# Delta rule: dealing the rows of a block's inverse out in turn over the partition groups

## The chip, the cores and the metric

The kernel runs on one core of one Trainium2 chip. The metric is the device time of one launch in microseconds (us); the runs shown agree within about 0.3%. Engines are called by the profile's names: PE (matrix products), DVE (vector), ACT (scalar), POOL (GpSimd) and SP, which here issues nearly all DMAs. PEld is PE's loading of weights.

## The reference

One layer of a hybrid encoder is applied to 512 prompt tokens and to eight requests of 16 tokens, 640 rows in all, in fp32. Each row goes through one wide input projection, then through two branches: forgetting attention with 8 heads, and a gated delta rule with 8 heads of 128 x 128 state. Both branches are projected, gated, merged, normalised and gated once more. The part that the change touches is the solve in the delta rule, per head and block of tokens:

```python
lmat = jnp.where(strict, jnp.einsum('nbhid,nbhjd->nbhij', kb, kc) * decay, 0.0)
amat = lmat + jnp.eye(c, dtype=lmat.dtype)
solve = functools.partial(lax.linalg.triangular_solve, left_side=True, lower=True)
u = solve(amat, vc * bc[..., None])
w = solve(amat, kb * jnp.exp(gc)[..., None])
```

`amat` is unit lower triangular. The kernel forms its inverse explicitly and multiplies by it.

## The kernel before, in words

**Stages.** The program has four stages: a front (input projection of the attention part and of gates), the attention stage, the delta-rule stage, and a tail (output projections, norm, last gate). In the profile the delta-rule stage runs from about 990 to 1600 us. PE is fed all the time by wide products: 128 x 128 weights against 320 columns, three products for one fp32 product (a high and a low part of each operand), recorded by `column` (L396, L397) and `pair` (L474). Between these, the heads' small products are slipped in, with PSUM tiles called `s`; the wide ones write tiles called `g`.

**One head of the delta rule** is a chain of Python generators. `gdn` (L901) transposes, normalises and forms `lt`, the scaled and masked key products (L974 on PE, L979 on DVE). `gdn_blocks` (L988) inverts the 32 x 32 blocks on the diagonal, 20 blocks a head (5 tiles of 128 tokens by 4). `gdn_feed` (L1015) reads the inverses back. `gdn_merge` (L1028) builds the 128 x 128 inverse `uu` from four blocks with small products (L1043, L1051, L1057, L1066, L1072; the DVE copies L1052, L1060 and L1074 lie between them). `gdn_chunks` (L1079) then runs the recurrence over the prompt's four tiles (`gdn_pro`, L1178: L1196 uses `uu`; L1188 and L1210 use the state `S`, which DVE writes in L1206; L1192 forms the right side `rp`) and the update of the eight requests (`gdn_dec`, L1132). `gdn_out` normalises and stores.

**The substitution (L1002 to L1008).** `lt`'s diagonal blocks are written to a DRAM tile `ld` (L993, four DMAs of 32 x 5 x 32), then read back as `lanes` (L998): a block's whole matrix, 1024 numbers, on each of four partitions, so 20 blocks fill 80 partitions. `x` (tile `sx`, 8 rows of 32 per partition) starts as the identity from an input `eye` (L996). A block has 32 rows of inverse; the four partitions of a block hold eight rows each: rows 0 to 7, 8 to 15, 16 to 23 and 24 to 31. Step j takes column j out of all eight slots with a multiply and a subtract (L1004, L1006): 31 steps, 62 DVE instructions a head. Row r of the inverse has nothing in column j before j reaches r, so many of these products are zeros. One DMA writes `x` to `xd` (L1012); `gdn_feed` reads it back as `u0`, 32 partitions per block (L1023, tile `u`). POOL copies it into `uu` (L1033), DVE transposes it into `m0` (L1035, tile `m`), and the merge begins with L1043 on PE.

**What sets the order.** Every engine runs its instructions in the order in which the kernel records them; the scheduler does not move them. The order is set while the kernel is written out, by a planner with a cost model. `saw` (L81) watches each recorded instruction and keeps a modelled clock for PE and a modelled time at which DVE, ACT and POOL are done: for DVE 0.17 us and 1.1 ns an element. After every few wide products `tick` (L125) lets each lane's generator go on, if its `yield` count of ticks has passed and the modelled time of what it recorded last lies behind the modelled clock of PE. So the number of elements in a DVE instruction decides how many wide products are recorded before the next piece of a head's chain. `yield -1` (L1008), after every second step of the substitution, lets the lane go on a little before DVE is done.

**Who else stands in these queues.** SP issues the weight loads (`wr`, L269), the sums of weights (`ws`, L291 and L301) and every head's loads. In this stage POOL issues the DMAs that complete the low part of the weights (`wl`, L342), between its copies. ACT makes `wh` and the negated high part.

Of the kernel before, what the change touches and what calls it, by code (L numbers as in the profile page):

```python
# [14 lines left out]
ALU = mybir.AluOpType  # L15
# [37 lines left out]
class Kernel:  # L53
# [934 lines left out]
    def gdn_blocks(self, h, kq, lt, qk, qg, kt, vr, cs):  # L988

        nc = self.nc  # L990
        for a in range(4):
            sl = slice(32 * a, 32 * a + 32)
            nc.sync.dma_start(out=self.ld[:, a].rearrange("t j i -> j t i"), in_=lt[sl, :, sl])  # L993
        yield 5
        x = self.zt([80, 8, 32], "sx")
        nc.sync.dma_start(out=x.rearrange("p c i -> p (c i)"), in_=self.i["eye"])  # L996
        lanes = self.zt([80, 32, 32], "lanes")
        nc.sync.dma_start(out=lanes.rearrange("p j i -> p (j i)"),  # L998
                          in_=bass.AP(self.ld.tensor, self.ld.offset, [[1024, 20], [0, 4], [1, 1024]]))
        yield 5  # L1000
        tmp = self.zt([80, 8, 32], "sx2")
        for j in range(31):  # L1002
            n = 31 - j
            nc.vector.tensor_tensor(out=tmp[:, :, 0:n], in0=x[:, :, j:j + 1].to_broadcast([80, 8, n]),  # L1004
                                    in1=lanes[:, j:j + 1, j + 1:32].to_broadcast([80, 8, n]), op=ALU.mult)
            nc.vector.tensor_tensor(out=x[:, :, j + 1:32], in0=x[:, :, j + 1:32], in1=tmp[:, :, 0:n], op=ALU.subtract)  # L1006
            if j % 2 == 1:
                yield -1  # L1008
        self.inv = h
        while self.fed < h - 2:  # L1010
            yield
        nc.sync.dma_start(out=self.xd[h % 2], in_=x.rearrange("p c i -> p (c i)"))  # L1012
        self.feeds["gens"].append(self.gdn_feed(h, kq, lt, qk, qg, kt, vr, cs))

    def gdn_feed(self, h, kq, lt, qk, qg, kt, vr, cs):  # L1015
# [1317 lines left out]
def _consts():  # L2333
    cb = np.zeros((P, C_N), np.float32)
    i = np.arange(P)
    blk = i // 16
    same = blk[:, None] == blk[None, :]
    le = i[None, :] <= i[:, None]
    cb[:, C_ID:C_ID + P] = np.eye(P)
    cb[:, C_MP:C_MP + P] = np.where(le, 0.0, NEG)  # L2340
    cb[:, C_MD:C_MD + P] = np.where(le & same, 0.0, NEG)
    cb[:, C_DP:C_DP + P] = np.where(le.T, 0.0, NEG)
    cb[:, C_DD:C_DD + P] = np.where(le.T & same, 0.0, NEG)
    cb[P - 1, C_SP:C_SP + P] = 1.0
    cb[:, C_SD:C_SD + P] = (i[:, None] % 16 == 15) & same
    cb[:, C_ONE:C_ONE + P] = 1.0
    cb[:, C_EO:C_EO + 2] = blk[:, None] % 2 == np.arange(2)[None, :]
    cb[:, C_S4:C_S4 + 32] = (i[:, None] % 32) == np.arange(32)[None, :]
    cb[:, C_G4:C_G4 + 4] = i[:, None] == 32 * np.arange(4)[None, :]
    smask = np.ones((32, T), np.float32)  # L2350
    t = np.arange(T)
    smask[0:8, (t >= NPT) & (t % 16 == 0)] = 0.0
    smask[8:16, ((t < NPT) & (t % P == 0)) | ((t >= NPT) & (t % 16 == 0))] = 0.0
    smask[16:32] = 0.0
    eye = np.zeros((20, 4, 8, 32), np.float32)
    for c in range(4):
        for j in range(8):
            eye[:, c, j, 8 * c + j] = 1.0
    return cb, smask, eye.reshape(80, 256)


def _layout(a):
# [43 lines left out]
    for b in gate[Kernel.GATES:]:  # L2406
# [24 lines left out]
    rowb[0:8, 3], rowb[8:32, 3] = 1.0, -1.0  # L2431
    rowb = np.tile(rowb, (4, 1))
    cb, smask, eye = _consts()
    arr = {"w": w, "xT": x.T.reshape(KT, P, T), "pT": pp.T.reshape(2, P, T),
           "wsm": wsm.reshape(KT, P, 32).transpose(1, 0, 2), "kc": kc, "vc": vc, "lfr": lfr, "conv": conv,
# [38 lines left out]
```

## Time and profile before

| what | value |
|---|---|
| time, median of 3 runs | 2175.85 us (2170.36 to 2176.83) |
| the profiled execution's own time | 2173.18 us |
| its span, first to last instruction | 2171.3 us |
| granted TensorE clock, mean | 0.999 |
| PE busy | 2149.0 us, 99% of the span |
| DVE busy | 1566.0 us, 72% |
| ACT busy | 1007.3 us, 46% |
| POOL busy | 401.9 us, 19% |
| DMA | 452.65 MB, 208 GB/s in the mean |

The table's first rows are times of whole launches; the rows under them come from one profiled execution. "Busy" is the share of the span in which an engine ran an instruction. Idle time counts only on the engine that bounds the kernel.

### The profile page before, as it was taken

How to read it: one execution, taken by the hardware profiler on the slowest of the kernel's cores; microseconds unless marked ns; L12 is line 12 of the kernel's file. 1: busy time of each engine (PE TensorE's matmuls, PEld its weight loads, DVE VectorE, ACT ScalarE, POOL GpSimd, SP SyncE). 2: the span in 40 equal slices, each digit the busy share in tenths (PEclk: the TensorE clock that was granted, in tenths of full speed). 3: DMA queues.
4: the chain of work that ended last, by engine and by line, in shares of the span. 5: the costliest groups of instructions: out<-in, count | busy, mean ns of one | idle time of the engine just before them, and what ended most of it. 6: DMA issues, size and time to landing. Idle time of an engine off the chain costs nothing.

```text
span 2171.3 us, 41951 instructions
## 1 busy us (share of the span) xinstructions
PE 2149.0 (99%) x15438; PEld 2082.3 (96%) x15438; DVE 1566.0 (72%) x3207; ACT 1007.3 (46%) x2213; POOL 401.9 (19%) x596
## 2 busy tenths in 40 slices
PE   9999999999999999999999999999999999999998
PEld 7799999999999998899999999999999999999998
DVE  5877776767776565566478677766757787789987
ACT  4344443443444343353655566655443343354544
POOL 0022233323330101002334333332000000021100
PEclk9999999999999999999999999999999999999999
DMA  6356656666554899869978778878567656673465
GB/s 235 101 184 202 189 182 199 198 199 194 184 180 158 276 325 344 314 199 291 241 179 199 180 188 194 189 182 248 161 229 260 209 171 202 201 276 122 153 227 173
DMA packets 240670, 452.65 MB, mean 208 GB/s; under 512 B 38920, under 2 KB 122504, under 8 KB 240464
## 3 DMA queue, kind: packets, MB, share of 16 engines
q1 hardware_dynamic: 224912, 421.64, 59.5%
q0 software_dynamic: 15552, 28.32, 8.0%
q8 instruction: 122, 2.00, 0.4%
q14 instruction: 84, 0.69, 0.1%
HBM read 353.48 MB, written 96.38 MB: 207 GB/s over the span
## 4 chain that ended last, share of the span: by engine, by line
PE 91%; DVE 3%; DMA 3%; ACT 1%; SPq 0%; issue 0%; POOL 0%; ACTq 0%; DVEq 0%; POOLq 0%
PE g L474 44%; PE g L396 18%; PE g L397 18%; PE g L440 2%; PE s L974 1%; PE s L742 1%; PE s L813 1%; PE s L773 1%; DMA ws138b<-ws 0%; PE s L440 0%; PE s L1168 0%; DMA nb<-rd 0%; DVE sx L1006 0%; DVE sx L1004 0%; PE s L726 0%
## 5 line engine op out<-in xcount | busy, mean ns | idle before, releaser
L329 ACT CAST wh<-wr 128x512 fp32r<-128x512 f32 x624 | 381.2, 619 | 288.7 <-PE g L474 109.5
L335 DVE TENSOR_TENSOR wl<-wr,wh 128x512 fp32r<-128x512 f32 x516 | 358.3, 708 | 183.5 <-ACT wh L329 173.7
L474 PE MATMUL g<-xh,wh 128*128 128x320 f32 (+1 forms) x1296 | 402.9, 311 | 2.7 <-ACT m L1278 1.6
L474 PE MATMUL g<-xl,wh 128*128 128x320 f32 (+1 forms) x1296 | 401.2, 310 | 0.6 <-DVE xl L371 0.6
L474 PE MATMUL g<-xh,wl 128*128 128x320 f32 (+1 forms) x1296 | 401.4, 310 | 0.0
L396 PE MATMUL g<-xh,wh 128*128 128x320 f32 (+1 forms) x960 | 313.0, 326 | 0.7 <-ACT wh L329 0.7
L396 PE MATMUL g<-xh,wl 128*128 128x320 f32 (+1 forms) x960 | 297.1, 309 | 0.8 <-DMA wl<-in_w 0.7
L396 PE MATMUL g<-xl,wh 128*128 128x320 f32 (+1 forms) x960 | 297.2, 310 | 0.4 <-DVE xl L371 0.4
L397 PE MATMUL g<-xh,wh 128*128 128x320 f32 x960 | 297.3, 310 | 0.0
L397 PE MATMUL g<-xl,wh 128*128 128x320 f32 x960 | 297.0, 309 | 0.0
L397 PE MATMUL g<-xh,wl 128*128 128x320 f32 x960 | 296.7, 309 | 0.0
L474 PEld LDWEIGHTS g<-xh,wh 128*128 128x128 f32 x1296 | 243.9, 188 | 4.3 <-ACT m L1278 2.1
L474 PEld LDWEIGHTS g<-xl,wh 128*128 128x128 f32 x1296 | 243.7, 188 | 1.1 <-DVE xl L371 1.1
L474 PEld LDWEIGHTS g<-xh,wl 128*128 128x128 f32 x1296 | 244.1, 188 | 0.0
L474 PE MATMUL g<-t,wh 128*128 128x320 f32 (+1 forms) x1088 | 241.4, 310 | 0.0
L335 DVE TENSOR_TENSOR wl<-sr,wh 128x512 fp32r<-128x512 f32 x200 | 147.9, 759 | 98.6 <-ACT wh L329 97.6
L295 POOL TENSOR_TENSOR ws<-ws 128x171 f32<-128x171 f32 (+2 forms) x152 | 116.7, 768 | 541.5 <-DMA ws<-in_w 535.7
L396 PEld LDWEIGHTS g<-xh,wh 128*128 128x128 f32 x960 | 180.9, 188 | 11.9 <-issue 7.1
L474 PEld LDWEIGHTS g<-t,wh 128*128 128x128 f32 x1088 | 181.9, 188 | 0.6 <-issue 0.3
L396 PEld LDWEIGHTS g<-xh,wl 128*128 128x128 f32 x960 | 180.6, 188 | 1.4 <-DMA wl<-in_w 1.0
L397 PEld LDWEIGHTS g<-xh,wh 128*128 128x128 f32 x960 | 181.0, 189 | 0.9
L396 PEld LDWEIGHTS g<-xl,wh 128*128 128x128 f32 x960 | 180.9, 188 | 1.0 <-DVE xl L371 1.0
(440 smaller groups left out, 4148.8 us busy)
## 6 DMA issues: line engine op xcount, KB each, us to landing
wr<-in_w SPq DMA_DIRECT2D x252, 512.0 KB
wl<-in_w POOLq DMA_DIRECT2D x108, 256.0 KB, 5.8
kc<-in_kc SPq DMA_DIRECT2D x32, 512.0 KB
vc<-in_vc SPq DMA_DIRECT2D x32, 512.0 KB
sr<-in_w SPq DMA_DIRECT2D x25, 512.0 KB
ws<-in_w SPq DMA_DIRECT2D x96, 128.0 KB
sb<-in_w SPq DMA_DIRECT2D x80, 128.0 KB
md<-m SPq DMA_DIRECT2D x32, 320.0 KB
```

The lines of the kernel that those rows point to most:

```text
L295: nc.gpsimd.tensor_tensor(out=o, in0=x, in1=y, op=op)
L329: nc.scalar.copy(out=hi, in_=src)
L335: nc.vector.tensor_tensor(out=lo, in0=src, in1=hi.bitcast(F32), op=ALU.subtract)
L396: nc.tensor.matmul(ps[0], whl[w], xhl[o][:, a], start=(first and x == 0), stop=(last and x == 2))
L397: nc.tensor.matmul(ps[1], whl[w], xhl[o][:, b], start=(first and x == 0), stop=(last and x == 2))
L440: nc.tensor.matmul(ps, x[:, sl], w, start=(s == 0 and n == 0), stop=(s == 15 and n == 2))
L474: nc.tensor.matmul(ps, a[:, w], b, start=(k == 0 and n == 0 and not more), stop=(k == last and n == 2), skip_group_check=True)
L742: nc.tensor.matmul(ops[:, 0:P], vn[:, kb, :], pT[:, kb * P:(kb + 1) * P], start=(kb == 0), stop=(kb == i))
L773: nc.tensor.matmul(s1[32 * j:32 * j + 32, :], self.qpad[:, 2 * j + par, :], kc[:, (j % 2) * NPT:(j % 2 + 1) * NPT], start=(par == 0), stop ...
L813: nc.tensor.matmul(od[32 * j:32 * j + 32, 0:P], self.ppad[:, c, 2 * j + par, :], vc[:, o:o + P], start=False, stop=(par == 1 and c == 3), ...
L974: nc.tensor.matmul(pp[:, o:o + 256].rearrange("p (a b) -> p a b", a=2), kq[:, 0, x], kq[:, :, x], start=True, stop=True)
```

## The change

Row r of a block's inverse moves from partition group r // 8, slot r % 8, to group r % 4, slot r // 4. The rows are dealt out in turn. Then, in step j, the rows that have begun (r <= j) fill the first j // 4 + 1 slots in every group, and the two DVE instructions treat only these slots. The count of instructions stays at 62 a head. The elements per partition of one pass over the 31 steps go from 8 x 496 = 3968 to 1560 (a sum of (j // 4 + 1) x (31 - j)).

The partitions are ordered group first, then block, so that each group's 20 partitions lie together. The identity in `eye` and the pattern with which `lanes` is read follow that. `xd` keeps its layout in DRAM (a block's 32 rows in order), so what reads it is unchanged; but since a partition's slots are now every fourth row, the write takes four DMAs, one a group, each with 160 pieces of 32 numbers (128 B), instead of one with 80 rows of 1 KB.

```diff
-                          in_=bass.AP(self.ld.tensor, self.ld.offset, [[1024, 20], [0, 4], [1, 1024]]))
+                          in_=bass.AP(self.ld.tensor, self.ld.offset, [[0, 4], [1024, 20], [1, 1024]]))
         yield 5
         tmp = self.zt([80, 8, 32], "sx2")
         for j in range(31):
             n = 31 - j
-            nc.vector.tensor_tensor(out=tmp[:, :, 0:n], in0=x[:, :, j:j + 1].to_broadcast([80, 8, n]),
-                                    in1=lanes[:, j:j + 1, j + 1:32].to_broadcast([80, 8, n]), op=ALU.mult)
-            nc.vector.tensor_tensor(out=x[:, :, j + 1:32], in0=x[:, :, j + 1:32], in1=tmp[:, :, 0:n], op=ALU.subtract)
+            m = j // 4 + 1
+            nc.vector.tensor_tensor(out=tmp[:, 0:m, 0:n], in0=x[:, 0:m, j:j + 1].to_broadcast([80, m, n]),
+                                    in1=lanes[:, j:j + 1, j + 1:32].to_broadcast([80, m, n]), op=ALU.mult)
+            nc.vector.tensor_tensor(out=x[:, 0:m, j + 1:32], in0=x[:, 0:m, j + 1:32], in1=tmp[:, 0:m, 0:n],
+                                    op=ALU.subtract)
             if j % 2 == 1:
                 yield -1
         self.inv = h
         while self.fed < h - 2:
             yield
-        nc.sync.dma_start(out=self.xd[h % 2], in_=x.rearrange("p c i -> p (c i)"))
+        xd = self.xd[h % 2]
+        for a in range(4):
+            nc.sync.dma_start(out=bass.AP(xd.tensor, xd.offset + 32 * a, [[1024, 20], [128, 8], [1, 32]]),
+                              in_=x[20 * a:20 * a + 20])
...
-    eye = np.zeros((20, 4, 8, 32), np.float32)
+    eye = np.zeros((4, 20, 8, 32), np.float32)
     for c in range(4):
         for j in range(8):
-            eye[:, c, j, 8 * c + j] = 1.0
+            eye[c, :, j, 4 * j + c] = 1.0
```

The planner's model counts fewer elements, so from the first head's substitution on it records the instructions of the delta-rule stage in another order; before that and after that stage the order is the same on every engine, and each PE instruction is there as often as before. Three places are shown. Rows give the source line, the operation, the tiles (out<-in) and the shape. In the changed kernel's rows the lines of the substitution are one higher than before (L1005 and L1007 for L1004 and L1006), and the lines behind it five higher (L1079 for L1074).

**DVE, head 5's merge.** The row for L1074 is the copy that completes `uu` of head 5; above it stand steps of head 6's substitution, whose first waits for `lanes`. Before:

```order
L1004 TENSOR_TENSOR sx_17586<-sx,lanes 80x8x25
L1006 TENSOR_TENSOR sx<-sx,sx_17586 80x8x25
L1004 TENSOR_TENSOR sx_17586<-sx,lanes 80x8x24
L1006 TENSOR_TENSOR sx<-sx,sx_17586 80x8x24
L880 SCALAR_TENSOR_TENSOR cy<-strip,taps,cy 128x664
L1004 TENSOR_TENSOR sx_17586<-sx,lanes 80x8x23
L1006 TENSOR_TENSOR sx<-sx,sx_17586 80x8x23
L1004 TENSOR_TENSOR sx_17586<-sx,lanes 80x8x22
L1006 TENSOR_TENSOR sx<-sx,sx_17586 80x8x22
L1074 TENSOR_SCALAR uu_11303<-s 64x4x64
```

The same place in the changed kernel:

```order
L1005 TENSOR_TENSOR sx_17546<-sx,lanes 80x2x25
L1007 TENSOR_TENSOR sx<-sx,sx_17546 80x2x25
L1005 TENSOR_TENSOR sx_17546<-sx,lanes 80x2x24
L1007 TENSOR_TENSOR sx<-sx,sx_17546 80x2x24
L1005 TENSOR_TENSOR sx_17546<-sx,lanes 80x3x23
L1007 TENSOR_TENSOR sx<-sx,sx_17546 80x3x23
L1005 TENSOR_TENSOR sx_17546<-sx,lanes 80x3x22
L1007 TENSOR_TENSOR sx<-sx,sx_17546 80x3x22
L1079 TENSOR_SCALAR uu_11303<-s 64x4x64
```

In both kernels ten steps of head 6, 20 instructions, stand between head 5's L1060 and L1074. They are narrower now, and two convolution steps (L880) that stood among them before have moved ahead of the merge.

**DVE, head 7's substitution begins.** Its first step waits for `lanes`; splits of weights and operands (L335, L371) and the recurrence of head 6 (L1192, L1206) stand between its steps. Before:

```order
L1004 TENSOR_TENSOR sx_18608<-sx,lanes 80x8x31
L1006 TENSOR_TENSOR sx<-sx,sx_18608 80x8x31
L1004 TENSOR_TENSOR sx_18608<-sx,lanes 80x8x30
L1006 TENSOR_TENSOR sx<-sx,sx_18608 80x8x30
L1192 SCALAR_TENSOR_TENSOR rp<-s,negc,vr 128x128
L335 TENSOR_TENSOR wl<-wr,wh 128x512
L371 TENSOR_TENSOR xl<-ogr,xh 128x640
L1004 TENSOR_TENSOR sx_18486<-sx,lanes 80x8x29
L1006 TENSOR_TENSOR sx<-sx,sx_18486 80x8x29
```

In the changed kernel:

```order
L1197 SCALAR_TENSOR_TENSOR rp<-s,negc,vr 128x128
L1005 TENSOR_TENSOR sx_18568<-sx,lanes 80x31
L1007 TENSOR_TENSOR sx<-sx,sx_18568 80x31
L1005 TENSOR_TENSOR sx_18568<-sx,lanes 80x30
L1007 TENSOR_TENSOR sx<-sx,sx_18568 80x30
L335 TENSOR_TENSOR wl<-wr,wh 128x512
L371 TENSOR_TENSOR xl<-ogr,xh 128x640
L1005 TENSOR_TENSOR sx_18568<-sx,lanes 80x29
L1007 TENSOR_TENSOR sx<-sx,sx_18568 80x29
L1005 TENSOR_TENSOR sx_18568<-sx,lanes 80x28
L1007 TENSOR_TENSOR sx<-sx,sx_18568 80x28
L1211 SCALAR_TENSOR_TENSOR S<-S,gl,s 128x128
```

The first step now stands behind L1192 (L1197), and the state update L1206 (L1211) stands behind the first four steps. How far a load stands ahead of its first use has changed too. In the order in which the kernel records its instructions over all engines, so many wide products of PE stand between:

| head | 0 | 1 | 2 | 3 | 4 | 5 | 6 | 7 |
|---|---|---|---|---|---|---|---|---|
| first and last step, before | 221 | 210 | 193 | 187 | 180 | 164 | 137 | 301 |
| first and last step, changed | 177 | 166 | 153 | 144 | 121 | 121 | 114 | 239 |
| load of `lanes` and first step, before | 18 | 16 | 36 | 19 | 39 | 40 | 20 | 43 |
| load of `lanes` and first step, changed | 18 | 22 | 42 | 24 | 29 | 43 | 24 | 18 |
| load of `u` and L1043, before | 60 | 75 | 90 | 69 | 60 | 96 | 74 | 49 |
| load of `u` and L1043, changed | 55 | 52 | 36 | 74 | 84 | 40 | 66 | 89 |

**SP, head 5's inverse goes out and comes back.** Before:

```order
L269 DMA wr<-in_w 128x1024
L1012 DMA xd_135<-sx 80x256
L1023 DMA u_17317<-xd_135 128x5x32
L269 DMA wr<-in_w 128x1024
L1176 DMA out_sts<-st 128x1024
```

The same place in the changed kernel:

```order
L1181 DMA out_sts<-st 128x1024
L1016 DMA xd_135<-sx 160x1x32 x4
L1222 DMA out_stp<-S 128x128
L1103 DMA og<-sgf_181 128x640
L301 DMA ws144S_252<-ws 128x171
L301 DMA ws144b<-ws 128x171
L301 DMA ws144S_253<-ws 128x171
L301 DMA ws144S_255<-ws 128x171
L884 DMA out_conv<-tail 128x27
L1028 DMA u_17302<-xd_135 128x5x32
L269 DMA wr<-in_w 128x1024
```

Four writes stand where one stood, and seven other DMAs have come between the write and the read, with the next weight load behind the read.

## The prediction

> **What bounds the kernel now.** I read the page's head first, then the time by stage, PE's waits, and the timelines around the one place where the substitution reaches PE.
>
> ```profile
> PE 2149.0 (99%) x15438; PEld 2082.3 (96%) x15438; DVE 1566.0 (72%) x3207; ACT 1007.3 (46%) x2213; POOL 401.9 (19%) x596
> PE 91%; DVE 3%; DMA 3%; ACT 1%; SPq 0%; issue 0%; POOL 0%; ACTq 0%; DVEq 0%; POOLq 0%
> ```
>
> PE is busy for 99% of the span and carries 91% of the chain that ended last. DVE, whose work is cut, carries 3%. The table by stage (busy time and count of PE, PEld, DVE, ACT, POOL, then granted clock, DMA share, GB/s):
>
> ```profile
> 110.00:660.00 550.00, 548.87 (x3739) 548.08 (x3739) 400.12 (x529) 228.65 (x426) 161.10 (x160) 1.00 0.61 193
> ...
> 1060.00:1600.00 540.00, 536.30 (x4149) 512.88 (x4148) 382.95 (x1213) 305.35 (x837) 162.01 (x278) 1.00 0.78 193
> ```
>
> The first row prices a wide product: 548.87 / 3739 = 0.147 us. The second is the stage that the change reorders. PE is idle there for 540 - 536.3 = 3.7 us, DVE for 157. PE's waits from 990 to 1600 us (total, times, longest):
>
> ```profile
> PE s L1196 <- DVE uu L1074: 1.9, 1, 1.9
> PE s L1072 <- issue: 0.9, 2, 0.7
> PE s L1168 <- DVE S L1206: 0.9, 1, 0.9
> PE g L396 <- DMA wl<-in_w: 0.7, 1, 0.7
> ```
>
> These 4.4 us are all that PE loses there. The first two meet in one event, in which the substitution is the cause:
>
> ```profile
> 1430.23 0.78 SPq L998 DMA_DIRECT2D lanes<-ld  x1
> ...
> 1437.38 0.41 DVE L1004 TENSOR_TENSOR sx<-sx,lanes 80x248 f32<-80x248 f32 x1 [5.58 <-DMA lanes<-ld]
> ...
> 1447.01 0.42 DVE L1074 TENSOR_SCALAR uu<-s 64x256 f32<-64x256 f32 x1
> ...
> 1433.79 0.67 PE L1066 MATMUL s<-t,lt 64*64 64x64 f32 x8
> ...
> 1440.65 0.65 PE L1072 MATMUL s<-uu,t 64*64 64x64 f32 x8 [0.70 <-issue]
> ...
> 1447.48 0.49 PE L1196 MATMUL s<-vr,uu 128*128 128x128 f32 x2 [1.92 <-DVE uu L1074]
> ...
> 1447.50:1451.00 3.50, 3.50 (x15) 3.50 (x16) 3.40 (x8) 2.16 (x4) 0.17 (x1) 0.58 1.02 261
> 1451.00:1455.00 4.00, 4.00 (x31) 3.99 (x30) 3.65 (x15) 0.41 (x2) 0.69 (x1) 0.94 0.91 206
> ```
>
> Head 6's first step waits on DVE for `lanes`, 7.15 us after its issue. Ten steps of full width then stand ahead of head 5's L1074 (1437.38 to 1447.01), and PE idles 1.92 us at L1196, after 0.70 at L1072. In the last two rows the granted clock falls to 0.58 and 0.94: 3.50 x 0.42 + 4.00 x 0.06 = 1.7 us more. The event costs 0.70 + 1.92 + 1.7 = 4.3 us.
>
> **The change part by part.** *DVE's work.* The two lines of the substitution, and single steps of it:
>
> ```profile
> L1006 DVE TENSOR_TENSOR sx<-sx,sx 80x248 f32<-80x248 f32 (+30 forms) x248 | 76.3, 308 | 8.5
> L1004 DVE TENSOR_TENSOR sx<-sx,lanes 80x248 f32<-80x248 f32 (+30 forms) x248 | 75.4, 304 | 16.5 <-DMA lanes<-ld 11.4
> ...
> 1437.83 0.41 DVE L1006 TENSOR_TENSOR sx<-sx,sx 80x248 f32<-80x248 f32 x1
> 1438.28 0.40 DVE L1004 TENSOR_TENSOR sx<-sx,lanes 80x240 f32<-80x240 f32 x1
> ...
> 1116.16 0.16 DVE L1004 TENSOR_TENSOR sx<-sx,lanes 80x8 f32<-80x8 f32 x1
> ```
>
> From 8 to 248 elements an instruction goes from 0.16 to 0.41 us: 1.04 ns an element over a fixed 0.15, and starts lie 0.45 apart at 0.41, so 0.04 of gap. A head drops from 2 x (31 x 0.15 + 3968 x 0.00104) = 17.6 us to 2 x (31 x 0.15 + 1560 x 0.00104) = 12.5. Eight heads save 41 us of DVE's 383 in the stage. If two-level patterns cost no less than the full width, it is 0. Neither end reaches PE by itself: DVE has 157 us to spare there, and PE's only loss to these steps is the event. So 0 us directly.
>
> *The event at head 5's merge.* The order keeps the 20 instructions between L1060 and L1074, but they hold 457 elements a pass in place of 2120: 20 x 0.19 + 2 x 457 x 0.00104 = 4.8 us; they took 9.6 with two convolution steps. L1074 then ends 7.15 + 4.8 + 0.4 = 12.4 us after the load's issue. PE reaches L1196 after 69 wide products, 10.1 us, plus some 2.2 of small ones (L1066 and L1072 at 0.67 and 0.65, the rest transposes and L1051): 12.3. The wait falls from 1.92 to about 0.1, and with it the low clock: **-4.3 us**; -2.4 if 1.9 us of it stay.
>
> *New short distances.* The reordering makes its own. Head 7's first step now comes 18 wide products (2.6 us) behind its `lanes`, where 43 stood, so DVE will sit there. Behind it wait L335, L371 and, for PE's L1188, head 6's L1206. DVE resumes 7.15 us after the issue and needs eight narrow instructions (8 x 0.22), a split of 0.69, one of 0.82 and L1206:
>
> ```profile
> 1500.84 0.69 DVE L335 TENSOR_TENSOR wl<-wr,wh 128x512 fp32r<-128x512 f32 x1 [0.38 <-ACT wh L329]
> 1501.46 0.82 DVE L371 TENSOR_TENSOR xl<-ogr,xh 128x640 fp32r<-128x640 f32 x1
> ...
> 1075.98 0.87 PE s L926 x8
> ```
>
> That makes 7.15 + 1.8 + 1.5 + 0.3 = 10.7. PE arrives after 48 wide products, 7.1 us, and small ones of 0.11 each (the last row), about 2.4: 9.5. **+1.2 us**; 0 if `lanes` lands in 5.2 us, as head 1's did (1124.73 to 1129.92, below), and 4.3 if the clock drops as before. At head 5, L1043 stands 40 wide products (5.9 us) behind the load of `u`:
>
> ```profile
> 1124.73 0.79 SPq L998 DMA_DIRECT2D lanes<-ld  x1
> ...
> 1129.92 0.41 DVE L1004 TENSOR_TENSOR sx<-sx,lanes 80x248 f32<-80x248 f32 x1 [1.57 <-DMA lanes<-ld]
> ...
> 1119.87 0.41 SPq L1023 DMA_DIRECT2D u<-xd  x1
> ...
> 1126.04 1.38 POOL L1033 COPY uu<-u 32x160 f32<-32x160 f32 x4 [7.02 <-DMA u<-xd]
> ```
>
> The load took 6.2 us there, and the transpose L1035 some 0.3: **+0.5 us**, between 0 and 4.3. Head 2 has 36 (5.3 us), with eight small products between (some 1.2), so 0. POOL's L1033 waits for the same load with issues of `wl` queued behind it. They are recorded at least 64 wide products (9.4 us) before PE uses them, 66 before the change, and land in:
>
> ```profile
> DMA to landing us min/median/max: 3.6/5.8/9.2
> ```
>
> 3.6 us of delay is covered in the median case; more would cost PE the excess. I take 0.
>
> *The write of `xd` in four pieces.* The nearest rows are the one write and the four of `ld`, which have the same 160 pieces of 128 B:
>
> ```profile
> 1116.56 0.33 SPq L1012 DMA_DIRECT2D xd<-sx  x1
> ...
> 1068.59 2.00 SPq L993 DMA_DIRECT2D ld<-lt  x4
> ```
>
> SP spends 2.0 us for 0.33, some 13 us over eight heads. Behind them stand weight loads that run three tiles ahead, so 0; without that cover it is at most 1.7 us a head. The load of `u` waits for four landings instead of one, and the next `wr` load stands behind it on SP. Seven other DMAs now lie between, so I take 0 here too. [...]
>
> *Sum.* 2173.18 - 4.3 + 1.2 + 0.5 = 2170.6 us on the profiled execution. That execution lies 2.7 us below the median of the runs (2175.85), so the forecast is **2173.3 us**, a change of -0.1%. With the ends (-4.3 and -1.1, the idle time that the reordered part has beside the event; -2.4 + 4.3 + 4.3) it lies between 2170.5 and 2182.1.
>
> The clock's share of these prices rests on the 0.58 row. [...]
>
> **The rivals.** *Slower: late loads under a tighter plan.* Where DVE, POOL and then PE wait in order for `u` or `lanes`, each such place costs up to the event's 4.3 us. Three of them (head 7's `lanes`, L1043 of heads 5 and 2) in place of the old one give 2173.2 + 2 x 4.3 + 2.7 = 2184.5. It decides from about two and a half such events on (the old 4.3 and the 6.5 of 0.3%). For it speaks that three of eight distances shrink; against it, that in the trace heads 0 and 1 had DVE waiting for `lanes` too, and PE lost at most 0.2 us there.
>
> *Faster: the reordered part loses nothing any more.* The wait for `wl` lies ahead of it, so 3.7 + 1.7 = 5.4 us: 2173.2 - 5.4 + 2.7 = 2170.5, -0.25%. For it speaks that the substitution ends some 5 us earlier in each head; against it, that the wait for L1206 (0.9) has nothing to do with the width, and that the plan passes the 5 us on to PE's order.
>
> *The change doesn't save DVE time*, because short instructions cost the fixed part anyway or the pattern costs more: the event stays, 2175.9. Against it stands the straight line from 0.16 to 0.41.
>
> **How the numbers follow.** A measurement of this kernel can tell about 0.3% (6.5 us) from no change. Forecast 0.70 (range of its own 2169 to 2178), slower rival 0.08, faster rival 0.14, no saving 0.08. The faster rival lies near the edge, so some 0.06 of it counts as faster, with 0.04 from the forecast's tail: faster 0.10. Slower: 0.08. Same: 0.82. The range for all, 2168 to 2181, leaves out the slower rival's worst and the runs' own spread of 6 us beyond it.
>
> **What would show it.** Right: L1004 and L1006 together near 110 us instead of 151.7, PE's busy time in the stage within 5 us, L1196's wait for L1074 gone, new waits at L1188 or L1043. Wrong: several stretches with a clock under 0.9, or PE waits for `wl` behind L1033. The forecast fails if the stage's idle time grows past 10 us, or if anything outside it moves, where the order is the same.

## The result and the profile after

The changed kernel takes 2195.93 us (median of five runs, 2194.47 to 2196.93); the kernel before, beside it, takes 2173.35 us (2170.36 to 2176.83). The ratio is 1.0104, 95% interval 1.009 to 1.0118: **slower by 1.0%, 22.6 us**. The forecast was 2173.3 with a range up to 2181, so it was wrong in its sign and in its range. The head of the page of the profile after (its execution took 2194.47 us, its span is 2192.7 us, the mean granted clock 0.994):

```profile
PE 2159.0 (98%) x15438; PEld 2088.9 (95%) x15438; DVE 1525.3 (70%) x3207; ACT 1006.3 (46%) x2213; POOL 401.7 (18%) x596
```

DVE's work did fall, 1566.0 to 1525.3 us. The two lines of the substitution, in the view by line:

```profile
L1007 DVE TENSOR_TENSOR sx<-sx,sx 80x60 f32<-80x60 f32 (+24 forms) x248 | 56.1, 226 | 8.5
L1005 DVE TENSOR_TENSOR sx<-sx,lanes 80x60 f32<-80x60 f32 (+24 forms) x248 | 55.0, 222 | 32.5 <-DMA lanes<-ld 21.8 <-DMA ws144S<-ws 5.0
```

They take 111.1 us where they took 151.7. But the idle time ahead of L1005 has doubled, 16.5 to 32.5. The stage in one window from 1060 to 1680 us, in the kernel before (busy time and count of PE, PEld, DVE, ACT, POOL, then granted clock, DMA share, GB/s):

```profile
1060.00:1680.00 620.00, 615.66 (x4688) 591.55 (x4688) 442.08 (x1332) 337.77 (x906) 162.01 (x278) 1.00 0.77 201
```

and after:

```profile
1060.00:1680.00 620.00, 603.23 (x4543) 576.29 (x4542) 385.03 (x1302) 329.86 (x894) 159.82 (x278) 0.98 0.74 194
```

PE got through 145 fewer products in the same time. It was idle for 620 - 603.23 = 16.8 us instead of 4.3. The trace's record of the granted clock has four stretches at half speed there, 3.41, 3.41, 10.24 and 3.41 us; half of their sum, 10.2 us, is lost work (before: one stretch of 3.41, 1.7 us). Idle time and clock together are 27.0 against 6.0, that is 21.0 us more (0.4 us of it is counted twice, because the longest stretch begins 0.8 us before PE goes on). The spans differ by 21.4, so the loss lies in this stage. PE's waits from 990 to 1680 us (total, times, longest), of the kernel after:

```profile
PE s L1071 <- DVE t L1057: 7.8, 2, 3.9
PE s L1201 <- DVE uu L1079: 3.9, 1, 3.9
PE s L1173 <- DVE og L1123: 2.1, 1, 2.1
```

L1057, L1065 and L1079 are the copies of a head's merge on DVE (L1052, L1060, L1074 before). Three stalls of 3.9 us are waits for such a copy. One of them, on SP, DVE and PE in turn, with the stretch of low clock behind it:

```profile
1308.95 0.67 SPq L998 DMA_DIRECT2D lanes<-ld  x1
...
1316.34 0.19 DVE L1005 TENSOR_TENSOR sx<-sx,lanes 80x31 f32<-80x31 f32 x1 [5.93 <-DMA lanes<-ld]
...
1317.02 0.18 DVE L1007 TENSOR_TENSOR sx<-sx,sx 80x30 f32<-80x30 f32 x1
1317.24 0.28 DVE L1057 TENSOR_SCALAR t<-s 32x128 f32<-32x128 f32 x1
...
1317.58 1.11 PE L1071 MATMUL s<-t,lt 64*64 64x64 f32 x8 [3.88 <-DVE t L1057]
...
1316.80:1327.10 10.30, 9.52 (x43) 8.96 (x44) 9.10 (x39) 3.95 (x9) 2.16 (x7) 0.50 0.64 163
```

The load of head 4's `lanes` lands 7.4 us after its issue. DVE has nothing else in front of it and sits for 5.93 us. Head 3's copy L1057, for which PE waits, stands four narrow instructions behind the first step: it needs nothing of `lanes`, it is queued behind the wait. At head 0 (stall until 1135.5 us) the copy also stands behind a first step, which waited 5.95 us, but here 24 step instructions and five others (7.0 us) lie between the two. The third is the event that the prediction was built on, head 5's merge:

```profile
SPq L998 <- DMA ld<-lt: 1.8, 1, 1.8
...
1441.70 0.66 SPq L998 DMA_DIRECT2D lanes<-ld  x1
...
1450.47 0.19 DVE L1005 TENSOR_TENSOR sx<-sx,lanes 80x31 f32<-80x31 f32 x1 [4.97 <-DMA ws144S<-ws]
...
1455.21 0.42 DVE L1079 TENSOR_SCALAR uu<-s 64x256 f32<-64x256 f32 x1
...
1455.68 0.49 PE L1201 MATMUL s<-vr,uu 128*128 128x128 f32 x2 [3.88 <-DVE uu L1079]
...
1456.60:1460.10 3.50, 3.50 (x17) 3.50 (x16) 3.15 (x11) 1.72 (x5) 1.79 (x4) 0.52 0.71 221
```

(The view names a `ws` load as what released the first step; nothing in the step reads `ws`; of the two tiles that it reads, `sx` and `lanes`, `lanes` was issued last, and the record of its landing ends 8.68 us after the issue, 0.1 us before the step.) The first row is SP's wait: from 1439.9 us SP stood 1.8 us at the load of `lanes` because the write of `ld` had not landed. Measured from where SP reached the load, DVE's side (1.8 wait, 8.77 to the first step, 4.74 of steps, 0.42 of copy) takes 15.7 us; before, with rows of the prediction, it took 7.15 + 9.63 + 0.42 = 17.2. PE arrives 1455.68 - 3.88 - 1439.9 = 11.9 us after that point; before, 1447.48 - 1.92 - 1430.23 = 15.3. So DVE's side became 1.5 us shorter and PE's 3.4: the stall grew from 1.92 to 3.88. The waits for the two loads in the whole stage say the same. DVE and SP, kernel before:

```profile
DVE sx L1004 <- DMA lanes<-ld: 11.4, 4, 5.6
...
SPq L998 <- DMA ld<-lt: 1.2, 2, 0.8
```

and after:

```profile
DVE sx L1005 <- DMA lanes<-ld: 21.8, 5, 5.9
...
SPq L998 <- DMA ld<-lt: 8.5, 5, 3.1
```

With head 6's 4.97 us, which the view puts down to `ws`, DVE's waits for `lanes` after are 26.8 us. The stall at L1173 (2.14 us) is of another kind. The copy L1123 ends it, and from 1259.7 us on DVE had been at work, without a wait that the view shows, on steps, on other short instructions and, just ahead of L1123, on the 17 of a norm (3.0 us).

**A correction to the table of distances.** The table of wide products "between" two instructions, ahead of the prediction, was read from the finished program's instruction list, and that list isn't in the order in which the kernel is written: a kernel with the same order on every engine as before (the first experiment below) had other counts in it. The quoted rows of single engines are right, the table is not. Counted while the kernel is written out, 30 wide products (five ticks of six) stand between the load of `lanes` and the first step at every head, in both kernels. Between the load of `u` and L1035, the transpose that begins the merge, stand 42 to 48 in both, but 60 at head 4 of the changed kernel; between that load and L1043 stand 54 to 84 before and 54 to 90 after, and 66 at head 5 of the changed kernel instead of the table's 40. The prediction's 69 wide products from head 6's load of `lanes` to head 5's L1196 are 78, and were 96 before. What differs most (a negative number says that the next head's first step stands ahead of the merge):

| wide products, head | 0 | 1 | 2 | 3 | 4 | 5 | 6 | 7 |
|---|---|---|---|---|---|---|---|---|
| first to last step, before | 192 | 210 | 192 | 162 | 180 | 150 | 138 | 282 |
| first to last step, changed | 150 | 144 | 120 | 138 | 126 | 120 | 120 | 240 |
| this head's L1035 to the next head's first step, before | 12 | -12 | 96 | 60 | 96 | 60 | 108 | |
| the same, changed | 12 | 48 | 204 | 36 | 180 | 60 | 192 | |

### The profile page after: what moved, and what is told of

Read it like the earlier page. It is cut to its first block, busy times and chain, and to the rows that moved or that the text cites. A ratio compares the mean times of both kernels' runs of the same rounds, so it can differ in the third digit from the quotient of the medians.

```text
span 2192.7 us, 41996 instructions
## 1 busy us (share of the span) xinstructions
PE 2159.0 (98%) x15438; PEld 2088.9 (95%) x15438; DVE 1525.3 (70%) x3207; ACT 1006.3 (46%) x2213; POOL 401.7 (18%) x596
## 5 line engine op out<-in xcount | busy, mean ns | idle before, releaser
L335 DVE TENSOR_TENSOR wl<-wr,wh 128x512 fp32r<-128x512 f32 x516 | 359.4, 710 | 179.4 <-ACT wh L329 170.7
L335 DVE TENSOR_TENSOR wl<-sr,wh 128x512 fp32r<-128x512 f32 x200 | 148.0, 759 | 99.0 <-ACT wh L329 96.2
```

What stands on the lines that cost most here:

```text
L335: nc.vector.tensor_tensor(out=lo, in0=src, in1=hi.bitcast(F32), op=ALU.subtract)
```

## The experiments

The theory after the first look: the planner, told of fewer elements, writes a tighter order; the loads don't shorten with it; DVE then waits for `lanes` with copies behind it that PE needs. The rivals: the change's own body (four writes of `xd`, the new pattern of reading `lanes`, the two-level patterns on DVE); a queue other than DVE's. Line numbers in the experiments are shifted by up to nine against the kernel before. Each kernel's ratio is against runs of the kernel before on the same chip.

**Order apart from body.** The first kernel has the changed body, but the planner is told the old number of elements (`8 * n`), so that every engine's order is that of before. The second has the body of before, and the planner is told the new number.

```diff
-        self.busy[e] = self.wrote[names[0]] = ready + a + b * max(sizes)
+        self.busy[e] = self.wrote[names[0]] = ready + a + b * (self.told or max(sizes))
...
+            self.told = 8 * n                 (first; second: (j // 4 + 1) * n)
             nc.vector.tensor_tensor(...)      (the two instructions of a step)
+            self.told = None
```

> The changed kernel (narrow steps, new partition order, four writes of xd), but the planner is told the old widths, so every engine's order is that of the kernel before. Plan theory (the new order alone makes the stalls): 2168 to 2177 us, PE idle from 1060 to 1660 us under 6 us. DMA theory (slower read of lanes and four writes delay the chain whatever the order): 2185 to 2197, with the clock below full in several stretches again. If both share it: 2178 to 2185.

> The kernel before (full width, old partition order, one write), but the planner is told the narrow widths, so every engine's order is that of the changed kernel. Plan theory: at least as slow as the changed kernel, 2193 to 2210 us, since the full-width steps then stand in DVE's queue as well. DMA theory: 2171 to 2182.

Measured: 2174.42 us, 0.9999 (0.9989 to 1.0008), for the changed body in the old order; 2208.11 us, 1.0153 (1.0136 to 1.017), for the old body in the new order. PE's waits in the latter:

```profile
PE s L1068 <- DVE t L1054: 8.4, 2, 5.9
PE s L1170 <- DVE og L1120: 3.8, 1, 3.8
PE s L1198 <- DVE uu L1076: 3.1, 1, 3.1
```

Both as the plan theory had it. The order alone makes a loss, larger than the change's own, and the same copies are waited for; the narrow steps soften it (the copies stand behind the steps too). All of the changed body together, four writes and all, costs nothing in the old order. It is not free of late loads, though. DVE's waits for `lanes` in the first kernel, and what led to its one PE stall over 1 us, on DVE, ACT and PE in turn:

```profile
DVE sx L1006 <- DMA lanes<-ld: 26.6, 7, 8.8
...
1439.86 0.19 DVE L1006 TENSOR_TENSOR sx<-sx,lanes 80x31 f32<-80x31 f32 x1 [8.78 <-DMA lanes<-ld]
1440.64 0.17 DVE L865 COPY strip<-cvst 128x24 f32<-128x24 f32 x1
...
1440.90 0.85 ACT L877 ACTIVATE cy<-strip,taps 128x664 f32<-128x664 f32 x1 [6.83 <-DVE strip L865]
1441.77 0.37 ACT L1075 COPY t<-s 64x256 f32<-64x256 f32 x1
...
1442.24 0.65 PE L1079 MATMUL s<-uu,t 64*64 64x64 f32 x8 [3.01 <-issue]
```

DVE waits 26.6 us for `lanes`, as long as in the changed kernel (26.8), and the time is that of before. In this run a wait on DVE cost only where something that PE was about to need stood behind it, and that was two queues away: DVE's copy L865 stood behind the first step, ACT waited for that copy, and the `t` that PE needs stood behind it on ACT. The view shows no releaser for the stall, only "issue".

**The pattern of reading `lanes`.** Three kernels. The changed kernel with the partitions block first again (`lanes` read as before, the writes of `xd` from every fourth partition); the kernel before with group-first partitions, reads and one write; and the first experiment with partitions block first.

```diff
-                          in_=bass.AP(self.ld.tensor, self.ld.offset, [[0, 4], [1024, 20], [1, 1024]]))
+                          in_=bass.AP(self.ld.tensor, self.ld.offset, [[1024, 20], [0, 4], [1, 1024]]))
...
-                              in_=x[20 * a:20 * a + 20])
+                              in_=x[a:80:4])
```

> The changed kernel with its partitions block first, so that lanes is read with the old pattern (still four writes, new plan, same order). Plan theory: 2192 to 2198 us, as the changed kernel; the wait of DVE for lanes stays at 5 waits of 20 us in total. DMA theory: the read from issue to first step falls from 7.3 to 8.8 us back to 5.2 to 7.2, DVE's waits to about 11 us, and the time to 2180 to 2188.

> The kernel before with its partitions group first: lanes is read with the changed kernel's pattern, xd still leaves in one write of 1 KB pieces, full width, old plan and order. Plan theory: 2170 to 2177 us. DMA theory: the slower read alone costs 3 to 10 us, 2176 to 2184, with DVE's waits for lanes above 15 us.

> Narrow steps and four writes, planner told the old widths (order of the kernel before), partitions block first, so that lanes is read with the old pattern. If the parts add up as the runs so far say (new read pattern +8 us, narrow steps with four writes -8 us, both in the old order): 2165 to 2169 us. If instead PE's idle and low clock in the reordered part are all there is to win (5.4 us in the kernel before): 2169 to 2173. If the narrow steps only cover the slower read and are worth nothing by themselves: 2173 to 2177.

Measured: 2188.62 us, 1.0063 (1.0048 to 1.0079), for the changed kernel read block first; 2182.56 us, 1.0039 (1.0024 to 1.0054), for the old body read group first; 2172.73 us, 0.9999 (0.9991 to 1.0008), for narrow steps in the old order read block first. In the first two the plan theory's range was missed (2192 to 2198 and 2170 to 2177): the read itself costs time. In the third the parts did not add up to the 2165 to 2169 of their sum. DVE's waits for `lanes` in these three, in that order:

```profile
DVE sx L1005 <- DMA lanes<-ld: 16.4, 5, 5.2
```

```profile
DVE sx L1004 <- DMA lanes<-ld: 21.1, 7, 7.2
...
PE s L1067 <- DVE t L1053: 3.9, 1, 3.9
```

```profile
DVE sx L1006 <- DMA lanes<-ld: 15.1, 5, 6.7
```

With the same order, the group-first read makes DVE wait longer by about the same each time: 11.4 to 21.1 (before against the second), 16.4 to 26.8 (the first against the changed kernel), 15.1 to 26.6 (the third against the first experiment). By the kernel's own patterns the read is 80 pieces of 4 KB in both. So a part of the change that the prediction gave no price costs 0.4% in the new order (1.0063 to 1.0104) and 0.4% in the old order at full width (1.0039). With narrow steps in the old order it costs nothing (0.9999 both times): narrow steps give back there what the late load takes. And the new order costs 0.6% by itself, with block-first reads and narrow steps (0.9999 to 1.0063). The packets of this load can't be told apart from others of 4 KB, but the trace's record of landings tells the two reads apart: after a first entry at 1.1 to 1.3 us, a block-first load is reported in ten entries and a group-first load in four (where no later load shares the record). The last of them comes 6.4 us after the issue in the median (5.0 to 8.3) of the 24 block-first loads of these three pairs, and 8.2 us (6.0 to 9.9) in the group-first ones. What makes the group-first read late was not tested apart.

**The queue on DVE.** The changed kernel, with the copies of the merge on ACT instead of DVE. The planner still books them as DVE's, so that the order of everything else stays.

```diff
-        nc.vector.tensor_single_scalar(t1[32:64, :, 0:32], px[32:64, 0:P].rearrange(...), -1.0, op=ALU.mult)
+        self.booked = True
+        nc.scalar.mul(t1[32:64, :, 0:32], px[32:64, 0:P].rearrange(...), -1.0)
+        self.booked = False
```

(and so for the copies into `uu`)

> The changed kernel with the merge's three copies (L1052, L1060, L1074 of the kernel before) on ACT in place of DVE; the planner books them on DVE as before, so every other row of every engine keeps its place. Theory that DVE's queue is the cause (copies that PE needs stand behind a first step that waits for lanes): the three waits of 3.9 us at PE and the low clock after them go, 2172 to 2181 us. Rival that PE meets something late in any case (u, lt, or the products of the merge themselves): 2188 to 2196.

Measured: 2188.95 us, 1.0076 (1.0059 to 1.0092). The time is in the rival's range. PE's waits for the copies are small now, but another instruction of DVE comes in their place:

```profile
PE s L1197 <- DVE S L1213: 3.7, 1, 3.7
PE s L1177 <- DVE og L1127: 2.1, 1, 2.1
PE s L1074 <- ACT t L1058: 1.5, 1, 1.5
...
1449.85 0.28 DVE L1213 COPY S<-s 128x128 f32<-128x128 f32 x1
```

From 1441.9 to 1449.8 us DVE runs steps of one head's substitution (and two short instructions) without a gap, and the copy of the state, L1213, stands behind them. So the stalls at the merge copies were the queue's doing, as the theory says, but taking them out won back about a quarter of the loss only (1.0104 to 1.0076): whatever stands behind the substitution is next.

**The load earlier.** The changed kernel with nine ticks instead of five between the load of `lanes` and the first step (54 wide products instead of 30), and the same with block-first reads.

```diff
-        yield 5
+        yield 9
         tmp = self.zt([80, 8, 32], "sx2")
```

> The changed kernel with nine ticks in place of five between the load of lanes and the first step, so that the load stands 54 wide products ahead instead of 30. Theory that the wait for lanes in DVE's queue makes the stalls: DVE's waits for lanes fall from 21.8 us to under 4, 2172 to 2182 us. Rival (the order as a whole is too tight, u and the recurrence too): 2185 to 2196.

> The changed kernel with partitions block first and nine ticks between the load of lanes and the first step. If read pattern and distance add up: 2166 to 2174 us, at or under the kernel before. If other waits of the new order stay (copies behind u, L1123 ahead of the state update): 2176 to 2184.

Measured: 2183.35 us, 1.0044 (1.0031 to 1.0058), and 2178.71 us, 1.0025 (1.0016 to 1.0034). In the first:

```profile
DVE sx L1005 <- DMA lanes<-ld: 1.9, 2, 1.4
...
PE s L1163 <- DVE og L1123: 4.9, 2, 3.0
PE s L1048 <- DVE sx L1005: 2.8, 1, 2.8
```

The first time lies between the two ranges, the second in that of the rival. DVE hardly waits for `lanes` any more, and 0.6% of the 1.04% has gone. But the four ticks also move what else stands in the queues, so the 0.6% isn't the price of the waits alone; at the same order the earlier landing of the block-first read was worth 0.4%. What is left isn't a late load of `lanes`. In the second kernel the same wait for L1123 is there (the kind that the changed kernel has at L1173), and the window ahead of it shows DVE busy for 13.29 of 14.70 us with short instructions (steps, and the 17 of a norm, at 0.2 us apiece):

```profile
PE s L1163 <- DVE og L1123: 4.9, 2, 3.0
...
1258.00:1272.70 14.70, 11.76 (x95) 11.16 (x94) 13.29 (x61) 9.21 (x28) 6.33 (x7) 1.00 0.70 139
```

**The same in the old order.** To see whether an earlier load makes either of the two neutral kernels faster: the old order with narrow steps read block first, and the kernel before as it is, both with nine ticks.

> Narrow steps, block first, the planner counting the full width, and nine ticks instead of five between the load of lanes and the first step. Without the nine ticks this kernel stood at a ratio of 0.9999 and PE idled 2.3, 0.9 and 0.7 us in the stage. Theory (a late load of lanes makes the stalls; a loose order forgives the rest): DVE's waits for lanes fall below 4 us, PE's idle time in the stage to under 3 us, and the ratio stays within 0.998 to 1.000, since there were only some 4 us to win. Rival (the narrow steps give PE something once no load is late): 0.996 or less. Rival (a later first step only moves DVE's crowd to another place, as in the changed order, where 4.9 us of stalls stayed): 1.002 or more.

> The kernel before with nine ticks instead of five between the load of lanes and the first step, steps at full width. Theory: the 1.9 us wait for uu behind head 6's steps goes, and nothing else comes, 0.998 to 1.000; the same as the narrow kernel beside it, so that the width of the steps is worth nothing even where no load is late. Rival (width counts once no load is late): this one stays at 1.000 or above and the narrow one lies 0.3% or more below it. Rival (the full-width steps, begun four ticks later, end too late for the next head's inverse): new waits at u or uu, 1.002 or more.

Measured: 2189.29 us, 1.0072 (1.0061 to 1.0084), and 2179.45 us, 1.0026 (1.0016 to 1.0037). Both expectations of the theory fell. In the first kernel:

```profile
DVE sx L1006 <- DMA lanes<-ld: 2.6, 1, 2.6
DVE m L1042 <- DMA u<-xd: 12.6, 3, 8.2
...
PE s L1124 <- ACT ob L1119: 5.4, 1, 5.4
PE s L1050 <- DVE strip L865: 5.0, 1, 5.0
```

and in the second:

```profile
DVE sx L1004 <- DMA lanes<-ld: 0.2, 1, 0.2
...
PE s L1117 <- ACT ob L1112: 5.4, 1, 5.4
```

The waits for `lanes` went, as said, and new ones came. In the first kernel PE stands 5.0 us at head 0's merge, behind 8.2 us of DVE's wait for `u`. (The row names `strip` L865; that copy runs right behind the transpose of `u`.) In the second the same stall is 1.0 us: there `u` was issued at 1130.5 us instead of 1132.4, behind one write of `xd` (0.33 us of SP) instead of four (3.1). In both, PE stands 5.4 us at the last head's output, until 1651 and 1643 us: the last wide product of the stage had begun 5.7 us before, and the output's products are PE's next. The substitution's last line says how late the last head was. Its minimum, median and maximum in ns, then its first and last start, before and in the narrow kernel with nine ticks:

```profile
L1006 DVE TENSOR_TENSOR sx<-sx,sx x248: 170/298/766, 1082.8 to 1554.8; 80x248 f32<-80x248 f32 x4, 80x232 f32<-80x232 f32 x4, 80x216 f32<-80x216 f32 x4, 80x200 f32<-80x200 f32 x4
```

```profile
L1008 DVE TENSOR_TENSOR sx<-sx,sx x248: 170/212/798, 1083.5 to 1578.1; 80x60 f32<-80x60 f32 x12, 80x54 f32<-80x54 f32 x8, 80x66 f32<-80x66 f32 x8, 80x28 f32<-80x28 f32 x8
```

In the kernel before with nine ticks the last step starts at 1570.2 us. So it comes 15 and 23 us later than before, and four more ticks a head use up the room at the end. In the new order read block first with nine ticks it starts at 1548.6 us, and PE has no such wait there. That the nine ticks help only where the order leaves room at the end fits these rows; it was not tested by itself.

All kernels together. PE's idle time and the clock's loss (half of the time at half clock) are those of the stretch from 1060 to 1680 us of the profiled execution; the sum's excess is over the 6.0 us of before.

| order | steps | `lanes` read | ticks | ratio (95%) | PE idle, us | clock, us | excess | median over before, us |
|---|---|---|---|---|---|---|---|---|
| old | full | block first | 5 | 1 (before) | 4.3 | 1.7 | | |
| old | narrow | group first | 5 | 0.9999 (0.9989-1.0008) | 5.1 | 1.7 | 0.8 | -0.2 |
| old | narrow | block first | 5 | 0.9999 (0.9991-1.0008) | 3.9 | 0 | -2.1 | -0.8 |
| old | full | group first | 5 | 1.0039 (1.0024-1.0054) | 8.5 | 5.1 | 7.6 | 7.9 |
| old | full | block first | 9 | 1.0026 (1.0016-1.0037) | 10.6 | 3.4 | 8.0 | 6.3 |
| old | narrow | block first | 9 | 1.0072 (1.0061-1.0084) | 17.3 | 10.2 | 21.5 | 16.2 |
| new | narrow | group first | 5 | 1.0104 (1.009-1.0118), the change | 16.8 | 10.2 | 21.0 | 22.6 |
| new | full | block first | 5 | 1.0153 (1.0136-1.017) | 25.5 | 15.4 | 34.9 | 33.5 |
| new | narrow | block first | 5 | 1.0063 (1.0048-1.0079) | 10.7 | 6.8 | 11.5 | 14.0 |
| new, copies on ACT | narrow | group first | 5 | 1.0076 (1.0059-1.0092) | 11.1 | 6.8 | 11.9 | 15.5 |
| new | narrow | group first | 9 | 1.0044 (1.0031-1.0058) | 9.8 | 8.5 | 12.3 | 9.9 |
| new | narrow | block first | 9 | 1.0025 (1.0016-1.0034) | 9.7 | 3.4 | 7.1 | 5.2 |

The excess is of one execution and the difference of medians; they agree within 6 us in every row, so PE's idle time and its clock in this stage are the account of all of them. None beats the kernel before. The parts don't add: a wait costs by what it happens to meet.

## Why the prediction was wrong, by its own steps

**DVE's saving: right, and worth nothing by itself.** 41 us were forecast, 40.7 measured; in the old order they bring a ratio of 0.9999. The straight line of 0.15 us and 1.04 ns an element held for the two-level patterns (the 16 steps of 80x75 took 0.23 us in the median, 0.23 by the line).

**The event at head 5's merge, -4.3 us: wrong, and the main failed step.** Its first term held: the ten steps took 4.74 us, 4.8 forecast. Two others failed. The load that was to land "7.15" us after its issue took 8.77 to the first step, with SP late by another 1.8; PE's arrival "after 69 wide products", at 12.3 us, rested on the false table. Measured from the load's issue, the copy was done at 13.9 us instead of 12.4 and PE arrived at 10.1 instead of 12.3, so the stall grew to 3.88 where it was to vanish. What fell is that DVE's side of the race would shrink by more than PE's: the load's time did not shrink with the steps (7.15 us to the first step before, 8.77 after), and the wide products ahead of PE's arrival did (96 before, 78 after).

**New short distances, +1.2 and +0.5: the mechanism right, the places and the price wrong.** DVE does wait 3.45 us for `lanes` at head 7's first step, but PE has no wait at L1188 (L1193 now) or L1043 (L1048) in the changed kernel; those distances were readings of the same table. The stalls came at the merges of heads 0, 3 and 5, where copies stand behind a first step that waits, and at L1173, where a copy stands behind DVE's other work. Each cost 2.1 to 3.9 us of idle time and 1.7 to 5.1 of clock. The margin was in sight: rows of before showed DVE waiting four times for `lanes`, and the model in `saw` has no time for a DMA at all. Fewer elements had to move everything behind those waits closer.

**The pattern of `lanes`: no price was given.** The prediction took the new read for the old one, at 7.15 and 5.2 us. It lands about 1.8 us later in the median and costs 0.4% of the 1.04%.

**The four writes: right as to PE.** They took 4 x 0.75 = 3.0 us of SP a head, 2.0 forecast; in the old order the kernel with them stands at 0.9999. `u` came later (DVE's waits for it 8.8 to 14.1 us in the stage), without a wait of PE behind it in the changed kernel. With nine ticks in the old order there was one of 5.0 us, where the kernel with one write has 1.0, so the zero is no rule. POOL's late issues of `wl` cost PE 0.2 us, as good as the forecast zero.

**Chances.** The slower rival, late loads under a tighter plan, is what happened; it had 0.08 and a price of 2184.5. The price was low because an event cost 3.8 to 9.0 us instead of 4.3, and there were four. The chance was low because the rival was tied to three places of the table. That "the plan passes the 5 us on to PE's order" was written against the faster rival, and should have been counted for the slower one. Two of the prediction's signs of failure came: four stretches at half clock, and 16.8 us of idle time in the stage where 10 was the mark.

## What to carry to other kernels

Where a planner sets the order from modelled costs, a cheaper instruction is a change of the order: first change the model's number alone and the instruction alone, and time both. Such a plan is only as safe as the latencies that it doesn't model; before making it tighter, list the waits for loads on the in-order queue, and what another engine needs from behind each. A read rearranged with equal bytes and pieces isn't the same read until it is timed.

## What was not expected of the hardware

**Half clock beside short idle times.** In the changed kernel PE's four idle stretches of over 2 us in the stage (3.88, 2.14, 3.88 and 3.88 us) each went with a stretch at half clock, of 3.41, 3.41, 10.24 and 3.41 us; these began 0.36 and 1.21 us after PE's return, 0.81 us before it and 1.04 us after it. In the kernel before, the 1.92 us at L1196 went with one of 3.41 us, which began 0.55 us after. Over all traces here, each of the 15 idle stretches of PE of 2.98 us or more in the stage went with half clock for 3.41, 6.83 or 10.24 us, which began between 1.7 us before PE's return and 1.4 us after it. So did 12 of the 15 between 1.9 and 2.8 us, and of the shorter ones those of 1.84, 1.53 and 1.34 us; others of 1.46, 1.44 and 1.36 us did not, nor did the 1.65 us near 100 us in the kernel before (1.64 in the changed one). The same stall of 2.14 us met both fates. Behind it in the changed kernel, and around it in the kernel with the copies on ACT:

```profile
1272.30:1275.80 3.50, 3.50 (x16) 3.50 (x15) 3.23 (x14) 0.00 (x0) 0.00 (x0) 0.51 0.64 252
```

```profile
1268.00:1285.00 17.00, 16.24 (x108) 15.81 (x109) 13.37 (x52) 8.23 (x22) 3.80 (x7) 1.00 0.77 184
```

So the length of the idle time alone does not tell which stall goes with half clock, and what does was not shown. How long the half clock lasts is open too: three stalls of 3.88 us in one trace brought 3.41, 10.24 and 3.41 us. In the changed kernel an idle microsecond of PE cost about 1.6 (27.0 / 16.8).

**Reads of equal size.** 80 rows of 4 KB, each of 20 blocks read four times, made DVE wait 16.4 us in the stage with a block's four reads next to each other (ten entries in the record of landings), and 26.8 us with the four passes one after the other (four entries), at the same order of instructions; SP issued the second form faster, 0.66 us against 0.78. A write of 160 pieces of 128 B took SP 0.75 us, and one of 80 pieces of 1 KB 0.33.
